# Making the moving operand's upper part ahead of the squares, the silu and the stationary operand's upper part, in a one-core decoder layer

## The chip, the cores and the metric

The kernel runs on one core of one Trainium2 chip. Five engines of the core take part: TensorE (PE; its weight loads are listed as PEld), VectorE (DVE), ScalarE (ACT), GpSimd (POOL) and SyncE (SP, which here only issues transfers). Each engine works through its own instructions in the order in which the program holds them, and semaphores tell one engine that another is done. The metric is the device time of one execution in microseconds; lower is better.

## The reference, cut to what matters

The reference is one inference step of a decoder layer for a prompt of 2048 tokens and for 32 sample tokens, in float32: a mixer of gated linear attention and a state-space part, then a cross-attention to 256 memory rows, then a SwiGLU feed-forward part, each with a norm before and after.

```python
def decoder_layer(x, s_gla, s_ssm, conv_buf, mk, mv, lw):
    m, s_gla, s_ssm, conv_buf = mixer(rmsnorm(x, lw['ln_mix_pre']), s_gla, s_ssm, conv_buf, lw)
    h = x + rmsnorm(m, lw['ln_mix_post'])
    a = cross_attend(rmsnorm(h, lw['ln_xa_pre']), mk, mv, lw['w_xq'], lw['w_xo'])
    h = h + rmsnorm(a, lw['ln_xa_post'])
    hf = rmsnorm(h, lw['ln_ffn_pre'])
    f = (jax.nn.silu(hf @ lw['w_gate']) * (hf @ lw['w_up'])) @ lw['w_down']
    h = h + rmsnorm(f, lw['ln_ffn_post'])
    return h, s_gla, s_ssm, conv_buf
```

The change concerns the dense products behind the mixer: `w_out`, the scores and values of the cross-attention (with weights folded beforehand), `w_gate` and `w_up`, and `w_down`.

## The kernel before, in words

**Products of three.** A float32 operand is split into an upper part, a copy of it in the type `fp32r`, and a lower part, the rest. ScalarE makes the upper part with a copy, VectorE the lower part with a subtraction that reads the upper one. `three` (lines 135 to 137) multiplies upper by upper, upper by lower and lower by upper: three matmuls for each block of 128 rows of contraction.

**Seven products for eight.** Each big product is cut in quarters, and seven products of sums of quarters give the four results (Winograd's form of Strassen's method). One such product is a **step** here: 12 matmuls with a contraction of 512, or 9 where it is 384. The stationary side of a step comes from a **unit** (class `Unit`): it loads a raw tile `raw`, VectorE makes sums `sum` (line 1650), ScalarE the upper part `s` (line 1668), VectorE the lower part, again `s` (line 1670). The moving side is kept in seven **places**, one for each product, made of **pieces** (class `Pieces`): a transfer issued by SP into a staging tile `st` (three of them; lines 1778 and 1795), the upper part on ScalarE (`larger`, line 1739, tile `r`), the lower part on VectorE, or on GpSimd for some (`smaller`, line 1743, tiles `r` or `e`); `smaller` then issues the load that lies three pieces ahead. A place takes two pieces.

**Passes.** `passes` lists nine passes of steps: `o`, `s`, `v` (mixer output, scores, values), three of `g` (gate and up for three blocks of rows) and three of `d` (down). The places stay for a whole pass and all units run past them. At the change from one pass to the next the seven places are made anew: while the last unit of a pass runs, one piece follows each step, and while the first unit of the next pass runs, again one piece follows each step. So there are nine stretches with 14 pieces each, and no pieces in between; in the first one seven of the 14 are made ahead of the loop.

**The order of the work.** `order` lists the steps by hand. For each step the loop of the function issues, in this order: the matmuls; the evacuation `evs` of the bank of PSUM (a copy on ScalarE for three of the seven products and the last, an addition on VectorE for the others: lines 1848 and 1850, 1977 and 1981, 1995 and 2002, 2047 and 2049); the functions in `later`, which are the squares of a finished half row (lines 1854 and 2056) or the silu (line 1982), and read what VectorE has just added; `part(e + 4)`, which gives VectorE the lower part for the step three ahead, and then the sum and ScalarE the upper part `s` for the step four ahead; `larger` of the piece; `tick`, the next bit of the norms and transposes of finished rows; and `smaller` of the piece. `pin` fixes this order on each engine. Some work is left loose (the sample rows' attention, line 1429, with its loads `sraw`, line 1418) and is set in between by the scheduler.

Of the kernel before, what the change touches and what calls it, by code (L numbers as in the profile page):

```python
# [42 lines left out]
def hymba_kernel(ctx: ExitStack, tc: tile.TileContext, a: dict, o: dict, dbg: dict | None = None):  # L43
# [1502 lines left out]
    def stage():  # L1546
        return pst.tile([P, 1024], F32, name="st", bufs=3)
# [269 lines left out]
    def rows(j, m):  # L1817
        return slice((2 * j + m) * P, (2 * j + m + 1) * P)
# [151 lines left out]
    def evac_gate(sg, w):  # L1970
        def ev(name, ps):
            i = AT[KEEP.get(name, name)]
            if i not in sg:
                sg[i] = pg.tile([P, 384], F32, name="sg", bufs=5)
            t = sg[i][:, 0:w]
            if name in KEEP:
                nc.scalar.copy(t, ps[:, 0:w])
            elif name == "C21":
                nc.scalar.activation(t, ps[:, 0:w], AF.Silu)
            else:  # L1980
                nc.vector.tensor_tensor(t, ps[:, 0:w], t, op=ALU.add)
                later.append(lambda: nc.scalar.activation(t, t, AF.Silu))
        return ev

    def evac_up(sg, w, blk, u):
        t3 = {}
        js = BLOCKS[blk]
        n = len(js)
        og = pg.tile([P, 1536], F32, name="og")[:, 0:n * 512].rearrange("p (j q c) -> p j q c", q=4, c=P)
        by = lambda x: x[:, 0:n * P].rearrange("p (j c) -> p j c", c=P)  # L1990

        def ev(name, ps):
            if name in KEEP:
                t = t3[KEEP[name]] = pg.tile([P, 384], F32, name="t", bufs=3)
                nc.scalar.copy(t[:, 0:w], ps[:, 0:w])
                return
            i = AT[name]
            s = sg[i]
            t = ps
            if name != "C21":  # L2000
                t = t3[name]
                nc.vector.tensor_tensor(t[:, 0:w], ps[:, 0:w], t[:, 0:w], op=ALU.add)
            nc.vector.tensor_tensor(og[:, :, i], by(t), by(s), op=ALU.mult)
            if w > n * P:
                nc.vector.tensor_tensor(s_f[:, 2 * u + i // 2, i % 2], t[:, n * P:w], s[:, n * P:w], op=ALU.mult)
            if name == "C21":
                if w > n * P:
                    there[0] = u + 1
                nc.gpsimd.dma_start(out=aT[js[0]:js[0] + n, :, u].rearrange("j p c -> p j c"), in_=og.rearrange("p j q c -> p j (q c)"))
        return ev  # L2010
# [116 lines left out]
    work = [(k, g, len(gs) - n) for k, (_, _, gs) in enumerate(passes) for n, g in enumerate(gs)]  # L2127
    begins = [n == 0 or work[n - 1][0] != k for n, (k, _, _) in enumerate(work)]
    XG, GD = 3, 3 + len(BLOCKS)

    def pieces_of(k):
        kind, i, _ = passes[k]
        if kind == "g":
            return pieces_g(k, i)
        if kind == "d":
            return pieces_w(k, a["w_down"], wT, *PARTS[i])
        return pieces_w(k, *{"o": (a["w_out"], wX[0]), "s": (flat2(wqk), wX[1]), "v": (flat2(wvo), wX[2])}[kind], 0, 4)
# [9 lines left out]
    def enter(k):  # L2147

        nonlocal pg, pd
        kind, i, _ = passes[k]  # L2150
        rate[:] = RATES[kind]
        if kind == "o":
            gain_row(px, "ln_mix_post")
            for u in range(4):
                aux.append(weight_sums(lambda n, u=u: flat2(wqk)[n, u], wX[1], u))
        if kind == "s":
            for u in range(4):
                aux.append(weight_sums(lambda n, u=u: flat2(wvo)[n, u], wX[2], u))
        if kind == "v":
            gain_row(px, "ln_xa_post")  # L2160
        if kind == "g":
            if i == 0:
                rctx.close()
                pg = fctx.enter_context(tc.tile_pool(name="pg", bufs=1, reuse_waits="tile"))

                pg.tile([P, 1536], F32, name="og")
            for u in range(NU):
                if u % (len(BLOCKS) - 1) == i:
                    aux.append(weight_sums(lambda n, u=u: a["w_down"][n, u], wT, u))
            if i + 1 == len(BLOCKS):  # L2170
                aux.append(samples_down())
        if kind == "d" and i == 0:
            fctx.close()
            pd = ctx.enter_context(tc.tile_pool(name="pd", bufs=1, reuse_waits="tile"))
            pd.tile([P, D], F32, name="m")
            pd.tile([P, D], F32, name="ga")
# [16 lines left out]
    def before_loads(k):  # L2193

        nonlocal rd
        kind, i, _ = passes[k]
        if kind != "g" or i + 1 < len(BLOCKS):
            drain(aux)
        if kind == "g" and i + 2 == len(BLOCKS):
            pin()  # L2200
            drain(back)
            pin(True)
            rd = ctx.enter_context(tc.tile_pool(name="rd", bufs=1, side="right", reuse_waits="tile"))
# [30 lines left out]
    coming = None  # L2234
    parted = 0

    for what in "sFsFsLFsFsFUsUFsUFsUPPFPPs":
# [4 lines left out]
        elif what == "L":  # L2242
            now = pieces_of(0)
# [28 lines left out]
    for e, (n, i) in enumerate(order):  # L2272
        k, g, left = work[n]
        kind, b, gs = passes[k]
        if i == 0:
            cur = n
            if begins[n]:
                if coming:
                    now, coming = coming, None
                enter(k)  # L2280
            held[n] = now
            w = now.w
            if kind == "g":
                if g[1] == 0:
                    sg = {}
                evs[n] = evac_gate(sg, w) if g[1] == 0 else evac_up(sg, w, b, g[0])
            elif kind == "d":
                h = {}
                if n + 1 == len(work):
                    for m in range(2):  # L2290
                        h[m] = stage()
                        nc.sync.dma_start(out=h[m], in_=hX[rows(g, m)])
                top = n in ys
                y = ys.pop(n, {})
                stays = left == 1 and b + 1 < len(PARTS)
                if stays:
                    ys[n + 1] = y
                evs[n] = evac_d(b, g, y, h, top, stays)
            else:
                evs[n] = quads(g, *{"o": (after_mix, True), "s": (after_scores, False), "v": (after_values, True)}[kind])  # L2300
            if left == 2 and k + 1 < len(passes):
                before_loads(k)
                coming = pieces_of(k + 1)
        if i == 2 and n + 1 < len(work) and on_top(n + 1):

            ys[n + 1] = {}
            for m in range(2):
                ys[n + 1][m] = pd.tile([P, D], F32, name="y", bufs=6)
                nc.sync.dma_start(out=ys[n + 1][m], in_=yp[work[n + 1][1]][:, m * D:(m + 1) * D])

        nt = PARTS[b][1] if kind == "d" else 4
        w = held[n].w
        if i == 0:
            banks[n, "A"] = accA.tile([P, 512], F32, name="accA")
        if i == 1:
            banks[n, "B"] = accB.tile([P, 512], F32, name="accB")
        if i == 3:
            banks[n, "C"] = accC.tile([P, 512], F32, name="accC")
        ps = banks[n, {1: "B", 3: "C", 5: "C"}.get(i, "A")]
        while i not in held[n].full:  # L2320
            held[n].step()
        sh, sl = units[n].got[i]
        start = i in (0, 1, 3)
        for kt in range(nt):
            ks = slice(kt * P, (kt + 1) * P)
            three(ps[:, 0:w], sh[:, ks], sl[:, ks], *held[n].moving(i, kt), start and kt == 0, kt == nt - 1, not start)
        if left == 1:
            spent.add((k, i))
        evs[n](NAMES[i], ps)

        todo, later[:] = list(later), []
        for fn in todo:
            fn()
        part(e + ahead_)

        p = coming if work[cur][2] == 1 else now if begins[cur] else None
        if p:
            p.larger()
        tick()
        if p:  # L2340
            p.smaller()
        if kind == "d" or not coming and now.done() and (k != XG or samp2):
            due[1] += rate[1]
            while due[1] >= 10:
                due[1] -= 10
                step(aux)
        pin()
        due[0] += rate[0]
        while due[0] >= 10:
            due[0] -= 10  # L2350
            step(back)
        pin(True)
        if samp2 is None and k == XG and not posts:
            leave_attention()
# [99 lines left out]
```

## Time and profile before

| what | value |
|---|---|
| time, median of 3 runs | 2816.3 us (2814.36 to 2820.68) |
| time of the profiled execution | 2820.75 us |
| its span, from the first to the last instruction | 2819.0 us |
| PE, DVE, ACT, POOL busy | 2729.5, 2079.1, 1472.8, 536.8 us |
| chain that ended last | PE 75%, DVE 13%, ACT 5%, DMA 3%, issue 3%, POOL 1% |
| upper parts of pieces, line 1739 | 126, of which 98 are 128x1024 |
| upper parts of the stationary operand, line 1668 | 798 |

A row of a group gives what the instruction writes and reads, how many there are, their busy time, the mean of one and, behind the second bar, how long the engine stood idle before them and for whom. In the time line a bracket at the end of a row is the idle time of that engine just before, with the instruction whose end released it. Steps, stretches and engines are named below as in this section.

### The profile page before, as it was taken

The numbers are of one execution on the slowest core, as the hardware profiler recorded it, in microseconds if no ns is written. First come the engines' busy times: TensorE is split into PE (matmuls) and PEld (weight loads), VectorE is DVE, ScalarE is ACT, GpSimd is POOL, SyncE is SP. The second block draws the span as 40 slices with busy tenths as digits, with TensorE's granted clock in tenths as the row PEclk, the third lists the DMA queues.
The fourth block names the chain that finished last, engine by engine and source line by source line (L and its number), as shares of the span: only waits on it lengthen the run. The fifth ranks groups of instructions, "written<-read, shape, count | busy, mean of one in ns | idle before, by whom it ended". The sixth has DMA issues, their size and how long they took to land.

```text
span 2819.0 us, 41809 instructions
## 1 busy us (share of the span) xinstructions
PE 2729.5 (97%) x15207; PEld 2367.6 (84%) x15207; DVE 2079.1 (74%) x3831; ACT 1472.8 (52%) x2921; POOL 536.8 (19%) x722
## 2 busy tenths in 40 slices
PE   8999999999998999999899999999999999999998
PEld 8987888788886878878799888899998998788786
DVE  7676677776757787677888787667678878574776
ACT  5545554554546787777755434434445555353432
POOL 2142332321321321015321210001000001000011
PEclk9999999999999999999999999999999999999999
DMA  7345435343266785468864567775234436464765
GB/s 255 113 142 188 148 106 160 118 131 90 83 215 226 282 291 223 146 189 254 263 222 179 177 237 243 253 254 178 98 137 171 156 120 209 168 219 99 239 152 132
DMA packets 151102, 512.17 MB, mean 182 GB/s; under 512 B 18176, under 2 KB 29488, under 8 KB 137328
## 3 DMA queue, kind: packets, MB, share of 16 engines
q1 hardware_dynamic: 94560, 331.81, 36.0%
q0 software_dynamic: 44240, 152.82, 16.8%
q10 hardware_dynamic: 12096, 24.86, 2.7%
q8 instruction: 120, 1.97, 0.3%
q14 instruction: 86, 0.70, 0.1%
HBM read 365.76 MB, written 143.67 MB: 181 GB/s over the span
## 4 chain that ended last, share of the span: by engine, by line
PE 75%; DVE 13%; ACT 5%; DMA 3%; issue 3%; POOL 1%; DVEq 0%; ACTq 0%; SPq 0%; POOLq 0%
PE accA L135 9%; PE accA L136 9%; PE accA L137 9%; PE accC L135 5%; PE accC L136 5%; PE accC L137 5%; PE acc L135 5%; PE acc L136 5%; PE acc L137 5%; PE accB L135 2%; PE accB L137 2%; PE accB L136 2%; DVE s L1670 2%; DVE sum L1650 2%; ACT r L1739 1%
## 5 line engine op out<-in xcount | busy, mean ns | idle before, releaser
L135 PE MATMUL accA<-r,s 128*128 128x512 f32 (+2 forms) x1792 | 637.2, 356 | 19.0 <-ACT r L1739 7.2
L137 PE MATMUL accA<-r,s 128*128 128x512 f32 (+2 forms) x1792 | 629.1, 351 | 2.9 <-DVE s L1670 2.8
L136 PE MATMUL accA<-r,s 128*128 128x384 f32 (+2 forms) x1472 | 502.7, 342 | 2.4 <-DVE r L1743 2.4
L135 PEld LDWEIGHTS accA<-r,s 128*128 128x128 f32 x1792 | 339.2, 189 | 70.9 <-ACT r L1739 11.0
L1668 ACT ACTIVATE s<-sum 128x512 fp32r<-128x512 f32 (+1 forms) x456 | 282.5, 620 | 218.9 <-DVE sum L1650 105.0
L137 PEld LDWEIGHTS accA<-r,s 128*128 128x128 f32 x1792 | 339.7, 190 | 33.2 <-DVE s L1670 4.0
L135 PE MATMUL accC<-r,s 128*128 128x512 f32 (+2 forms) x896 | 318.8, 356 | 9.2 <-ACT s L1668 3.2
L1670 DVE TENSOR_TENSOR s<-sum,s 128x512 fp32r<-128x512 f32 (+1 forms) x456 | 306.8, 679 | 20.1 <-ACT s L1668 19.8
L137 PE MATMUL accC<-r,s 128*128 128x512 f32 (+2 forms) x896 | 314.3, 351 | 0.0
L136 PEld LDWEIGHTS accA<-r,s 128*128 128x128 f32 x1472 | 279.0, 190 | 19.2 <-DVE r L1743 3.6
L1670 DVE TENSOR_TENSOR s<-raw,s 128x512 fp32r<-128x512 f32 (+1 forms) x342 | 233.7, 683 | 52.0 <-ACT s L1668 50.9
L136 PE MATMUL accC<-r,s 128*128 128x384 f32 (+2 forms) x736 | 251.3, 341 | 0.5 <-DVE r L1743 0.5
L1668 ACT ACTIVATE s<-raw 128x512 fp32r<-128x512 f32 (+1 forms) x342 | 213.3, 624 | 72.1 <-PE accC L137 49.8
L129 ACT ACTIVATE whi<-wraw 128x1024 fp32r<-128x1024 f32 (+2 forms) x140 | 128.9, 934 | 184.2 <-PE acc L136 104.5
L135 PEld LDWEIGHTS accC<-r,s 128*128 128x128 f32 x896 | 169.8, 189 | 37.2 <-ACT s L1668 7.8
L130 DVE TENSOR_TENSOR wlo<-wraw,whi 128x1024 fp32r<-128x1024 f32 (+2 forms) x140 | 156.2, 1127 | 48.0 <-ACT whi L129 47.3
L137 PEld LDWEIGHTS accC<-r,s 128*128 128x128 f32 x896 | 169.7, 189 | 14.9 <-DVE s L1670 0.2
L143 POOL TENSOR_TENSOR rs<-ms,nhalf 128x1 f32<-128x1 f32 (+4 forms) x125 | 111.0, 889 | 360.3 <-DVE ms L141 343.9
L135 PE MATMUL acc<-xhl,whi 128*128 128x512 f32 (+1 forms) x464 | 168.1, 363 | 8.3 <-ACT xhl L294 8.2
L137 PE MATMUL acc<-xhl,wlo 128*128 128x512 f32 (+1 forms) x464 | 164.3, 355 | 1.7 <-DVE wlo L130 1.7
L136 PE MATMUL acc<-xhl,whi 128*128 128x512 f32 (+1 forms) x464 | 164.1, 355 | 0.2 <-DVE xhl L295 0.2
L1650 DVE TENSOR_TENSOR sum<-raw 128x512 f32<-128x512 f32 (+1 forms) x228 | 156.4, 686 | 3.6
(696 smaller groups left out, 5857.9 us busy)
## 6 DMA issues: line engine op xcount, KB each, us to landing
raw<-in_w_gu_dram SPq DMA_DIRECT2D x66, 1024.0 KB, 4.9
wraw<-in_w_in_fm_dram SPq DMA_DIRECT2D x52, 512.0 KB, 3.6
wraw<-in_w_in_tm_dram SPq DMA_DIRECT2D x48, 512.0 KB, 3.9
st<-in_w_down_dram SPq DMA_DIRECT2D x37, 512.0 KB, 6.2
aT<-og POOLq DMA_DIRECT2D x22, 768.0 KB, 4.6
raw<-aT SPq DMA_DIRECT2D x16, 1024.0 KB, 6.3
out_y_dram<-y POOLq DMA_DIRECT2D x28, 512.0 KB, 6.1
yp<-y POOLq DMA_DIRECT2D x28, 512.0 KB, 6.6
```

Source lines behind the costliest of these rows:

```text
L129: last[0] = nc.scalar.activation(hi[:, cs], raw[:, cs], AF.Copy)
L130: nc.vector.tensor_tensor(lo[:, cs], raw[:, cs], f(hi)[:, cs], op=ALU.subtract)
L135: nc.tensor.matmul(ps, lhsT=wh, rhs=ah, start=start, stop=False, skip_group_check=more)
L136: nc.tensor.matmul(ps, lhsT=wh, rhs=al, start=False, stop=False, skip_group_check=more)
L137: nc.tensor.matmul(ps, lhsT=wl, rhs=ah, start=False, stop=stop, skip_group_check=more)
L143: nc.gpsimd.tensor_tensor(out=rs[:rows, :cols], in0=ms[:rows, :cols], in1=nhalf[:rows, :cols], op=ALU.pow)
L1650: nc.vector.tensor_tensor(t[out], x, y, op=o)
L1668: nc.scalar.activation(h3, v, AF.Copy)
L1670: return lambda: nc.vector.tensor_tensor(l3, v, f(h3), op=ALU.subtract)
L1739: nc.scalar.activation(hi, v, AF.Copy)
```

## The change

In each step of the nine stretches the piece's `larger` is issued right behind the evacuation, ahead of the functions in `later` and of `part`. `smaller` stays where it was. No instruction is added or removed by it.

```diff
         evs[n](NAMES[i], ps)
 
+        p = coming if work[cur][2] == 1 else now if begins[cur] else None
+        if p:
+            p.larger()
         todo, later[:] = list(later), []
         for fn in todo:
             fn()
         part(e + ahead_)
-
-        p = coming if work[cur][2] == 1 else now if begins[cur] else None
-        if p:
-            p.larger()
         tick()
         if p:
             p.smaller()
```

On ScalarE at the first stretch (pass `o`; `y<-accA` and `y<-accC` are evacuations, `mx,sq` a square, `s` the stationary operand's upper part, `r` a piece's):

```order
 L1848 COPY y<-accA 128x512
-L1668 ACTIVATE s<-sum 128x512
 L1739 ACTIVATE r_8234<-st 128x1024
+L1668 ACTIVATE s<-sum 128x512
+L1739 ACTIVATE r_8281<-st 128x1024
 L1854 ACTIVATE mx,sq_8256<-y 128x512
 L1668 ACTIVATE s<-sum 128x512
-L1739 ACTIVATE r_8286<-st 128x1024
```

The piece that stood behind the square and the next `s` stands ahead of both; the order of the others among themselves is the same.

On ScalarE in the last stretch, at the change to the third `d` pass, around the first square (`mx,sq`), before:

```order
L1668 ACTIVATE s<-sum 128x512
L1739 ACTIVATE r_25812<-st 128x1024
L2056 ACTIVATE mx,sq_25769<-y 128x512
L1668 ACTIVATE s<-sum 128x512
L1739 ACTIVATE r_25812<-st 128x1024
L1668 ACTIVATE s<-raw 128x512
L1739 ACTIVATE r_25858<-st 128x1024
L1668 ACTIVATE s<-raw 128x512
```

and with the change:

```order
L1739 ACTIVATE r_25807<-st 128x1024
L1668 ACTIVATE s<-sum 128x512
L1739 ACTIVATE r_25807<-st 128x1024
L2056 ACTIVATE mx,sq_25769<-y 128x512
L1668 ACTIVATE s<-sum 128x512
L1739 ACTIVATE r_25855<-st 128x1024
L1668 ACTIVATE s<-raw 128x512
L1739 ACTIVATE r_25855<-st 128x1024
```

Two pieces of one place now stand ahead of the square, with one `s` between them; before, the second stood behind the square and its `s`.

On PE the order of the steps is the same. One group of the loose work is set elsewhere: the five matmuls of the sample scores (`mx<-sraw,sqm`) in the stretch at the change to the second `g` pass. Before:

```order
L136 MATMUL accA<-r_17215,s 128x384
L137 MATMUL accA<-r_17215,s 128x384
L1429 MATMUL mx<-sraw,sqm 32x256 x5
L135 MATMUL accC<-r_17277,s 128x384
L136 MATMUL accC<-r_17277,s 128x384
```

and with the change:

```order
L137 MATMUL accC<-r_17272,s 128x384
L135 MATMUL accA<-r_17319,s 128x384
L1429 MATMUL mx<-sraw,sqm 32x256 x5
L136 MATMUL accA<-r_17319,s 128x384
L137 MATMUL accA<-r_17319,s 128x384
```

They stood ahead of the step into `accC` and now stand behind it and behind the first matmul of the next step.

## The prediction

> **What bounds the kernel now.** I read the table of stretches first, then the waits at the pieces' lines, then the time line at the worst places. Columns of the table: window and its length, busy us (and count) of PE, PEld, DVE, ACT and POOL, granted TensorE clock, DMA share, GB/s. The nine windows are the changes of pass; the tenth lies between two of them.
>
> ```profile
> span 2819.0 us, 41809 instructions
> ...
> 855.00:889.00 34.00, 26.47 (x79) 17.78 (x78) 22.34 (x29) 17.53 (x27) 1.44 (x1) 0.80 0.73 247
> 1012.00:1062.00 50.00, 45.16 (x208) 35.51 (x207) 45.45 (x63) 43.09 (x80) 12.89 (x16) 1.00 0.90 301
> 1186.00:1234.00 48.00, 45.99 (x215) 36.88 (x214) 41.05 (x61) 43.12 (x93) 2.49 (x5) 1.00 0.64 219
> 1354.00:1398.00 44.00, 36.14 (x173) 30.74 (x172) 38.69 (x67) 36.45 (x80) 17.49 (x27) 0.95 0.85 284
> 1741.00:1786.00 45.00, 41.41 (x279) 34.74 (x272) 35.39 (x55) 23.40 (x40) 0.76 (x1) 0.96 0.90 308
> 2095.00:2131.00 36.00, 30.11 (x187) 28.98 (x187) 29.25 (x49) 20.76 (x41) 0.74 (x1) 0.95 0.64 216
> 2351.00:2385.00 34.00, 28.39 (x155) 23.03 (x155) 28.48 (x43) 20.23 (x35) 10.17 (x9) 0.95 0.68 224
> 2481.00:2514.00 33.00, 31.71 (x139) 25.65 (x138) 30.53 (x40) 23.37 (x32) 1.06 (x2) 1.00 0.80 261
> 2630.00:2677.00 47.00, 42.74 (x179) 34.23 (x178) 39.27 (x53) 24.70 (x36) 1.42 (x2) 0.96 0.76 236
> 1100.00:1180.00 80.00, 80.00 (x387) 66.93 (x386) 52.05 (x91) 54.33 (x137) 8.62 (x16) 1.00 0.45 171
> ```
>
> Between changes PE is busy for 80.00 of 80 us: there PE bounds and nothing on ScalarE matters. The nine stretches last 371 us, and PE is busy for 328.1 of them (the column's sum), so 42.9 us are idle; and at a clock of 0.80, 0.95, 0.96, 0.95, 0.95 and 0.96 in six of them another 16 us or so are lost to half clock (34 x 0.20 = 6.8, 44 x 0.05 = 2.2, 45 x 0.04 = 1.8, 36 x 0.05 = 1.8, 34 x 0.05 = 1.7, 47 x 0.04 = 1.9). All that the change can win lies in these 59 us; it reaches only what hangs on the pieces. Which part that is, the views of lines 1739 (first rows) and 1743 (last two rows) tell: duration, what ScalarE idled for ahead of a piece, and who idled for it.
>
> ```profile
> L1739 ACT ACTIVATE r<-st x126: 239/1046/1110, 838.0 to 2673.5; 128x1024 fp32r<-128x1024 f32 x98, 128x512 fp32r<-128x512 f32 x21, 128x64 fp32r<-128x64 f32 x7
> ...
>   DMA st<-wX: 6.4, 4
>   DMA st<-in_w_down_dram: 3.8, 3
>   DMA st<-wT: 3.6, 6
>   DMA st<-xp: 1.8, 1
> ...
>   PE accA L135: 7.2, 7
> ...
>   ACT r L1739: 76.6, 62
> ...
>   PE accA L136: 9.6, 12
> ```
>
> VectorE and GpSimd stand idle for 76.6 us before lower parts because the upper part is not there yet, and PE waits 7.2 + 9.6 = 16.8 us directly, in 19 waits, for one or the other. ScalarE, on the other hand, waits for a piece's load in only 14 cases, 15.6 us (6.4 + 3.8 + 3.6 + 1.8).
>
> **The change, step by step.** It removes and adds nothing: the same copy of 1.05 us is issued earlier. What it moves past is seen in the third stretch (ScalarE, VectorE, PE in turn):
>
> ```profile
> 1228.51 0.60 ACT L1854 ACTIVATE mx<-y 128x512 f32<-128x512 f32 x1 [1.10 <-DVE y L1850]
> 1229.14 0.62 ACT L1668 ACTIVATE s<-sum 128x512 fp32r<-128x512 f32 x1
> 1229.66 1.04 ACT L1739 ACTIVATE r<-st 128x1024 fp32r<-128x1024 f32 x1
> ...
> 1228.99 0.68 DVE L1650 TENSOR_TENSOR sum<-sum,raw 128x512 f32<-128x512 f32 x1
> 1230.73 1.23 DVE L1743 TENSOR_TENSOR e<-st,r 128x1024 fp32r<-128x1024 f32 x1 [1.06 <-ACT r L1739]
> ...
> 1230.76 0.50 PE L135 MATMUL accA<-r,s 128*128 128x512 f32 x1 [0.49 <-ACT r L1739]
> 1232.02 0.50 PE L136 MATMUL accA<-e,s 128*128 128x512 f32 x1 [0.76 <-DVE e L1743]
> ```
>
> The piece stands 1.15 us behind the square's start (1229.66 - 1228.51), and the square itself waited 1.10 us for VectorE. If the load is there, the piece can run in that gap, at 1227.4. VectorE's order is unchanged, so its subtraction then follows its own sum, at 1229.7 in place of 1230.73: 1.06 us earlier, its whole wait. PE's first wait goes; the second shrinks, and together PE gets about 1.1 us. Where only the `s` copy stands ahead (1229.66 - 1229.14), it is 0.5 us. The cost moves to the square and `s`: they come 1.05 us later at most, but `s` is for the step four ahead, and a square's sum is read steps later.
>
> *Term 1, direct waits.* 19 waits come mostly in such pairs, so some ten places; one or two hang on the load. Nine places by 0.5 to 1.1 us are 4.5 to 9.9; I take **7 us**, nearer the row above, as most sit in steps with a square or silu.
>
> *Term 2, waits for a bank.* Where VectorE waits for a late piece, the next evacuation queues behind it. The last stretch shows that at its largest (same three engines):
>
> ```profile
> 2655.76 1.06 ACT L1739 ACTIVATE r<-st 128x1024 fp32r<-128x1024 f32 x1 [2.34 <-DMA st<-in_w_down_dram]
> 2658.71 0.60 ACT L2056 ACTIVATE mx<-y 128x512 f32<-128x512 f32 x1 [1.89 <-DVE y L2049]
> 2659.86 1.04 ACT L1739 ACTIVATE r<-st 128x1024 fp32r<-128x1024 f32 x1
> ...
> 2656.85 1.23 DVE L1743 TENSOR_TENSOR r<-st,r 128x1024 fp32r<-128x1024 f32 x1 [1.12 <-ACT r L1739]
> 2660.94 1.23 DVE L1743 TENSOR_TENSOR e<-st,r 128x1024 fp32r<-128x1024 f32 x1 [1.66 <-ACT r L1739]
> 2662.08 0.68 DVE L2049 TENSOR_TENSOR y<-accC,y 128x512 f32<-128x512 f32 x1
> ...
> 2662.91 0.52 PE L135 MATMUL accC<-r,s 128*128 128x512 f32 x1 [3.23 <-ACT s L1668]
> 2663.23 0.63 PE L136 MATMUL accC<-r,s 128*128 128x512 f32 x1
> 2663.66 0.63 PE L137 MATMUL accC<-r,s 128*128 128x512 f32 x1
> ```
>
> PE's wait of 3.23 us is put down to `s`, but `accC` was also being emptied until 2662.76. The piece at 2655.76 waits for its load and stays. The next one waited behind a square that waited for VectorE, which had waited for the first: by the new order it starts at about 2657.4 (behind one `s` of 0.6), is done before VectorE wants it, and VectorE saves its 1.66 us. PE gets 1.7 of the 3.23. Two more such waits end on ScalarE's own evacuations behind a piece:
>
> ```profile
> PE accC L135 <- ACT sg L1977: 3.0, 2, 2.1
> PE accC L135 <- ACT t L1995: 1.5, 1, 1.5
> PE mx L1429 <- DMA sraw<-in_cache_k_dram: 3.0, 1, 3.0
> ```
>
> Of their 4.5 us perhaps half goes, 2.3, since the silu or copy there waits for VectorE too: 1.7 + 2.3 = **4 us**, bounds 1 and 6.
>
> *Term 3, half clock.* At 2663.23 and 2663.66 matmuls start 0.43 us apart; that is how half the clock looks, and it follows the long wait. The stretch 1012:1062 idles for 4.84 us in shorter waits and stays at 1.00. Of the 16 us I take **3**; bounds 0 and 8 (half, as the first stretch's waits begin with loads). [...]
>
> *Term 4, the loose group.* PE's 3.0 us for `sraw` (last row above) stood ahead of a step of 12 matmuls that did not need it; that step now runs during the load, until the next one waits for its own piece. **2 us**, bounds -1 (the other sample loads come later) and 3.
>
> *Term 5, the charge.* A piece in front that waits for its load now holds the square, `s` and the next evacuation.
>
> ```profile
> 1051.14 0.61 ACT L1668 ACTIVATE s<-raw 128x512 fp32r<-128x512 f32 x1
> 1054.57 1.06 ACT L1739 ACTIVATE r<-st 128x1024 fp32r<-128x1024 f32 x1 [2.81 <-DMA st<-wX]
> ```
>
> Here `s` slips from 1051.14 to 1055.6, 4.5 us; PE needs it four steps on, 12 matmuls a step, so it is nearly covered. Fourteen such pieces each cost what follows at most 0.6 to 1.2 us of copies formerly done during the wait: 0 to 17 us if all reached PE; I take **3**, since only evacuations have no slack.
>
> *Term 6, absorption.* A gain of one step is lost where VectorE is simply full: 30.53 busy of 33 us in 2481:2514, 45.45 of 50 in 1012:1062. **3 us**, bounds 0 and 7.
>
> Sum: 7 + 4 + 3 + 2 - 3 - 3 = **10 us**. The profiled execution took 2820.75 us (span 2819.0 and 1.75 around it), 4.45 above the median of 2816.3; the same 10 us on the median give **2806 us**. With all bounds at their bad ends it is 4.5 + 1 + 0 - 1 - 17 - 7 = -19.5, at their good ends 9.9 + 6 + 8 + 3 = 27.
>
> **The rivals.** *A, VectorE or the loads are the bound of a change of pass (no difference).* With three staging tiles a load can only be issued when the piece three before it is subtracted, so an earlier piece just waits for its load, and VectorE's queue stays full. For it: the VectorE shares just named, DMA shares up to 0.90. Against it: 76.6 us of waits for the upper part against 15.6 us of ScalarE's for loads. Terms 1 to 3 then give about 4 and term 5 takes 2 back: 2814 us.
>
> *B, the queue blocks (slower).* One mechanism: the piece in front waits for `st`, and the evacuation behind it keeps `accC` or `accA` full. The place is the `wX` and `w_down` loads (the 2.81 and 2.34 us above). It decides once `s` is late by over three steps, 3 x 12 x 0.22 = 8 us (0.22 us from one matmul to the next is half of the 0.43 above), or an evacuation by over one, 2.6 us; 1.05 + 2.81 = 3.9 is past the second. With 1.2 us at each of 14 pieces, 17 us of waits less 7 for term 1, it is 10 us slower: 2826 us. [...]
>
> [...]
>
> The order of the instructions shows that the piece does move ahead, so that it does nothing is not a rival.
>
> **How the numbers follow.** Forecast 0.55, A 0.24, B 0.11, C 0.10. A measurement of this kernel tells 0.2% from no change, 5.6 us: faster means below 2810.7. Nearly all of C, 0.50 of the forecast and 0.05 of A lie there: 0.65. Slower is B, above 2821.9: 0.10. Within: 0.25. The forecast's own range is 2798 to 2812; for 8 in 10 it reaches into A and C: 2796 to 2817.
>
> **What would show it.** Right: the idle time of VectorE for line 1739 falls from 76.6 us to under 40; PE's 16.8 us at least halves; the wait of 3.23 us falls under 2; the clock of 855:889 rises above 0.85; the rows between changes stay as they are. Wrong: ScalarE's waits for `st` grow by as much as VectorE's fall (A), or PE waits for evacuations and `s` behind a piece that waits for its load (B). What would upset it all is that pieces become ready earlier and the load of three later does not.

## The result and the profile after

| | before | changed |
|---|---|---|
| median of 4 runs | 2815.33 us (2810.73 to 2820.68) | 2794.44 us (2789.85 to 2797.14) |
| ratio to before | 1 | 0.9919 [0.9907, 0.9931] |
| profiled execution | 2820.75 us, span 2819.0 | 2795.36 us, span 2793.6 |

The change makes the kernel 20.9 us faster, 0.8%. The forecast had the direction, but less than half of the size: 10 us, 2806 us, and even its wide range (2796 to 2817) ends 1.6 us above what was measured.

The page of the changed kernel, its span and the shares of the chain that ended last:

```profile
span 2793.6 us, 41826 instructions
...
PE 78%; DVE 11%; ACT 4%; issue 3%; DMA 3%; POOL 1%; DVEq 0%; POOLq 0%; SPq 0%; ACTq 0%
```

In the chain PE has gone from 75% to 78%, and VectorE from 13% to 11%.

**Where the time went.** To compare the stretches, each is cut in both traces at the same two instructions of VectorE (lower parts of the stationary operand, line 1670, which stand in the same place of the order in both). The table of windows gives for each its length, then PE's busy time, and behind the busy times of the other engines the granted clock. Before, the first stretch (change to `o`), the first of `g`, the last of `d`, and the sum over all nine:

```profile
865.30:909.30 44.00, 39.34 (x147) 29.86 (x147) 31.40 (x50) 25.91 (x52) 6.92 (x10) 0.86 0.54 183
...
1351.00:1415.10 64.10, 56.24 (x286) 50.27 (x285) 54.92 (x94) 48.59 (x103) 22.16 (x34) 0.95 0.77 256
...
2625.00:2679.40 54.40, 50.14 (x211) 40.32 (x210) 45.06 (x62) 25.52 (x37) 2.47 (x4) 0.97 0.73 222
sum 479.80, PE 439.79 PEld 366.35 DVE 397.43 ACT 312.81 POOL 68.91; mean PE 48.87 PEld 40.71 DVE 44.16 ACT 34.76 POOL 7.66
```

and the same with the change:

```profile
862.30:900.60 38.30, 35.62 (x147) 26.94 (x147) 31.13 (x51) 25.43 (x52) 6.16 (x10) 0.97 0.60 215
...
1336.60:1401.30 64.70, 57.15 (x286) 51.32 (x285) 54.40 (x93) 48.47 (x103) 23.70 (x34) 0.92 0.76 254
...
2604.80:2654.00 49.20, 48.25 (x212) 39.22 (x211) 44.71 (x62) 25.62 (x37) 3.37 (x4) 1.00 0.80 245
sum 459.20, PE 433.54 PEld 363.49 DVE 395.03 ACT 311.88 POOL 71.20; mean PE 48.17 PEld 40.39 DVE 43.89 ACT 34.65 POOL 7.91
```

All nine, from the same two tables (PE idle is length less PE busy):

| stretch | length, us | difference | PE idle, us | clock |
|---|---|---|---|---|
| `o` | 44.0 to 38.3 | -5.7 | 4.7 to 2.7 | 0.86 to 0.97 |
| `s` | 72.3 to 69.3 | -3.0 | 4.8 to 2.5 | 1.00, 1.00 |
| `v` | 54.3 to 51.7 | -2.6 | 2.0 to 0.3 | 1.00, 1.00 |
| `g`, first | 64.1 to 64.7 | +0.6 | 7.9 to 7.6 | 0.95 to 0.92 |
| `g`, second | 52.7 to 50.8 | -1.9 | 3.6 to 2.8 | 0.97 to 0.93 |
| `g`, third | 43.1 to 39.5 | -3.6 | 5.9 to 2.8 | 0.96, 0.96 |
| `d`, first | 53.5 to 53.8 | +0.3 | 5.6 to 4.7 | 0.97 to 0.94 |
| `d`, second | 41.4 to 41.9 | +0.5 | 1.3 to 1.3 | 1.00, 1.00 |
| `d`, third | 54.4 to 49.2 | -5.2 | 4.3 to 1.0 | 0.97 to 1.00 |
| sum | 479.8 to 459.2 | -20.6 | 40.0 to 25.7 | |

Of the 20.6 us, 14.3 are idle time of PE and 6.3 are busy time, of which 3.7 lie in the first stretch, where the clock rises. Of the 25.4 us between the two spans, 3.0 more lie ahead of the first cut, where executions differ by chance (the cut is at 865.2 in a second profile of the changed kernel, and at 861.3 in a kernel tried below that keeps the old order there), and 1.8 lie between the stretches; the medians leave 20.9. Three stretches gain nothing, in the second profile as in the first.

The view of line 1739 in the changed kernel, what ScalarE idled for ahead of a piece and who idled for it (us, times), and the last rows from the view of line 1743, the lower part:

```profile
  DMA st<-wT: 19.9, 18
  DMA st<-xp: 15.8, 9
  DMA st<-wX: 8.7, 6
  DMA st<-in_w_down_dram: 8.7, 4
...
  DVE r L1743: 24.1, 27
  POOL r L1743: 24.1, 6
...
  DVE e L1743: 6.2, 6
  PE accA L135: 5.8, 4
...
  ACT r L1739: 54.4, 39
...
  PE accA L136: 7.2, 10
```

Before, the waits for an upper part were these:

```profile
  DVE r L1743: 39.9, 45
  POOL r L1743: 25.9, 6
...
  DVE e L1743: 10.9, 11
```

VectorE's own waits fall from 50.8 to 30.3 us, GpSimd's six stay at 24.1. ScalarE's waits for loads of pieces grow from 15.6 us in 14 cases to 54.6 in 39 (the four rows, and 1.0 and 0.5 us in two more), the sign that was named for rival A, and yet the kernel is faster.

**The last stretch**, where the bank of `accC` had kept PE for 3.23 us. ScalarE, VectorE and PE in turn, with the change:

```profile
2634.89 1.06 ACT L1739 ACTIVATE r<-st 128x1024 fp32r<-128x1024 f32 x1 [4.83 <-DMA st<-in_w_down_dram]
...
2636.38 1.04 ACT L1739 ACTIVATE r<-st 128x1024 fp32r<-128x1024 f32 x1
2637.85 0.60 ACT L2056 ACTIVATE mx<-y 128x512 f32<-128x512 f32 x1 [0.42 <-DVE y L2049]
...
2635.99 1.23 DVE L1743 TENSOR_TENSOR r<-st,r 128x1024 fp32r<-128x1024 f32 x1 [0.55 <-ACT r L1739]
...
2638.33 1.22 DVE L1743 TENSOR_TENSOR e<-st,r 128x1024 fp32r<-128x1024 f32 x1
...
2640.29 0.47 PE L135 MATMUL accC<-r,s 128*128 128x512 f32 x1 [0.86 <-DVE y L2049]
2640.60 0.40 PE L136 MATMUL accC<-r,s 128*128 128x512 f32 x1
2640.83 0.40 PE L137 MATMUL accC<-r,s 128*128 128x512 f32 x1
```

The second piece starts 1.5 us behind the first, ahead of the square, where 4.1 lay between them before. VectorE's subtraction at 2638.33 waits for nothing (1.66 before), the bank comes free earlier, PE's wait is 0.86, and the matmuls behind it stand 0.23 us apart, not 0.43 (before, the trace's granted clock is 0.50 from 2663.18 to 2666.59). The first piece's wait for its load, now 4.83, kept nobody on PE.

**The first stretch** shows the busy time that went. PE before:

```profile
863.60 0.51 PE L135 MATMUL accA<-r,s 128*128 128x512 f32 x1 [1.34 <-ACT r L1739]
864.86 0.79 PE L136 MATMUL accA<-e,s 128*128 128x512 f32 x1 [0.76 <-DVE e L1743]
...
868.15 0.80 PE L135 MATMUL accC<-r,s 128*128 128x512 f32 x1 [0.79 <-ACT y L1848]
...
874.23 0.57 PE L136 MATMUL accA<-r,s 128*128 128x512 f32 x1
874.63 0.39 PE L137 MATMUL accA<-r,s 128*128 128x512 f32 x1
```

and with the change:

```profile
860.54 0.49 PE L135 MATMUL accA<-r,s 128*128 128x512 f32 x1 [1.79 <-ACT r L1739]
861.80 0.79 PE L136 MATMUL accA<-e,s 128*128 128x512 f32 x1 [0.76 <-DVE e L1743]
...
864.80 0.46 PE L136 MATMUL accC<-r,s 128*128 128x512 f32 x1
865.10 0.40 PE L137 MATMUL accC<-r,s 128*128 128x512 f32 x1
```

In both, the granted clock falls to 0.50 in the second wait of the same pair, at 864.36 us before and at 861.51 with the change. Before, one more wait followed, 0.79 us for ScalarE's evacuation, and matmuls stayed slow from 864.86 to 874.23, 9.4 us; with the change that wait is not there and they are slow from 861.80 to 864.80, 3.0 us. That this wait decides how long the slow spell lasts is not shown. In the second profile of the changed kernel, which lacks the wait too, the clock of this stretch is 0.93; and in a kernel tried below (the three stretches that gain nothing), which keeps the old order here and such a wait, it is 0.96:

```profile
865.10:907.40 42.30, 35.66 (x147) 27.33 (x146) 31.44 (x50) 25.84 (x52) 6.97 (x10) 0.96 0.53 191
```

With this higher clock and the old order PE is busy for 35.7 us in place of 39.3, but idle for 6.6 in place of 4.7, and the stretch is only 1.7 us shorter than before. So in this stretch about half of what the clock saves comes back as longer waits, and a loss reckoned from the clock alone overstates what the clock costs here.

### The profile page after: what moved, and what is told of

Same layout as the page of the kernel before. It is cut to its first block, busy times and chain, and to the rows that moved or that the text cites. A ratio compares the mean times of both kernels' runs of the same rounds, so it can differ in the third digit from the quotient of the medians.

```text
span 2793.6 us, 41826 instructions
## 1 busy us (share of the span) xinstructions
PE 2720.1 (97%) x15207; PEld 2362.1 (85%) x15207; DVE 2075.6 (74%) x3831; ACT 1472.2 (53%) x2921; POOL 540.1 (19%) x722
## 3 DMA queue, kind: packets, MB, share of 16 engines
q0 software_dynamic: 44240, 152.82, 16.8%
## 4 chain that ended last, share of the span: by engine, by line
PE 78%; DVE 11%; ACT 4%; issue 3%; DMA 3%; POOL 1%; DVEq 0%; POOLq 0%; SPq 0%; ACTq 0%
PE accA L135 10%; PE accA L136 10%; PE accA L137 10%; PE accC L135 5%; PE acc L135 5%; PE accC L137 5%; PE accC L136 5%; PE acc L136 5%; PE acc L137 5%; PE accB L135 3%; PE accB L137 3%; PE accB L136 3%; DVE s L1670 2%; DVE sum L1650 1%; PE mx L1863 1%
```

## The experiments

The theory behind the prediction is that a piece in front takes waits from VectorE and PE, and that it is charged for each load that ScalarE then waits for. The experiments put the new order into some stretches, move the piece past the one or the other, and make the loads later. Times are medians, ratios are to the kernel before on the same chip in the same set of runs (medians 2816.7, 2815.9 and 2816.6 us in the three sets).

### Half of the stretches each

```diff
-        if p:
+        soon = p and p.k < XG
+        if soon:
             p.larger()
         todo, later[:] = list(later), []
         for fn in todo:
             fn()
         part(e + ahead_)
+        if p and not soon:
+            p.larger()
```

This is the changed kernel with the new order in the changes to `o`, `s` and `v` alone; its counterpart has `p.k >= XG`, the six changes to `g` and `d`.

> The piece is issued in front only in the stretches at the changes into the passes o, s and v; in the six others it stays behind. Theory (each stretch wins what its late pieces cost, on its own): the two profiles lose 11.3 us between them in these three stretches (5.7, 3.1, 2.5), so 11 us faster than before, about 2804. Rival (the gain is that of the half clock, in the first and the last stretch): 6 us faster, 2809. Rival (some of the 21 us is the chance of the runs): under 5 us.

> The converse: in front in the stretches into the three g and the three d passes, behind in o, s and v. Theory: the profiles give 9.3 us here (g2 3.6, the last d 5.2, the second g 1.9, the other three lose 1.5 together), so 9 to 10 us faster than before, about 2806, and with the run beside it the two add up to the whole change, 20 to 22 us. Rival (half clock alone): 5 us, the last stretch. If they do not add up, a stretch's gain depends on the one before.

Measured: 2804.93 us, ratio 0.996 [0.9945, 0.9975], for `o`, `s`, `v`; 2805.98, 0.9964 [0.9949, 0.9978], for `g` and `d`. The gains, 11.8 and 10.7 us, add up to 22.5, what the whole brings. Cut as above, the first kernel's three stretches are 4.4, 2.7 and 2.5 us shorter, and in the second the gain lies in the second and third `g` and the last `d` (3.1, 3.2 and 5.7). The stretches that keep the old order are 0.8 us longer in sum in the first kernel and 0.6 shorter in the second, though one of them alone can differ by more (the last `d` of the first kernel is 2.4 shorter). So most of the gain is local to each stretch, and PE's wait for `sraw` (4.2 us in the first kernel, none in the second) goes with the change at `g` alone.

### The three stretches that gain nothing

```diff
-        soon = p and p.k < XG
+        soon = p and p.k in (XG, GD, GD + 1)
```

The new order stands only in the first change to `g` and the first two to `d`.

> The piece in front only in the stretches into the first g pass and into the first and second d pass, where the profiles of the whole change gain nothing (0.6, 0.4 and 0.5 us longer). Theory (VectorE's queue is full there, so an earlier piece only waits: term 6): between 2 us slower and 2 us faster than before. Rival (they gain as the others do, and the profiles of single executions hide it): 4 us or more faster.

Measured: 2814.37 us, 0.9991 [0.9983, 1.0], 2.3 us faster, just beyond what the theory allowed and short of the rival's 4. Those three stretches are 0.5 us shorter, 0.4 longer and 1.6 longer than before. There a third of the pieces moves ahead for next to nothing. The theory's reason, a full VectorE, does not tell these stretches from the others: in the table of windows before, VectorE is busy for 0.86, 0.82 and 0.90 of them, and for 0.87 of the changes to `s` and to `v`, which gain 3.0 and 2.6 us. What they show is this: in the first `g` and the first `d` PE's longest wait is for an evacuation by VectorE, and it stays (3.4 and 4.1 us before, 3.8 and 3.6 with the whole change); in the second `d` PE idles for only 1.3 us to begin with. Why those two waits stay was not tried. The whole again, beside it on the same chip:

> The changed kernel itself, timed beside the next one: 20 to 24 us faster than before.

Measured: 2795.65 us, 0.9923 [0.991, 0.9935]; the result repeats.

### Past the squares only, past `s` only

```diff
         p = coming if work[cur][2] == 1 else now if begins[cur] else None
+        part(e + ahead_)
         if p:
             p.larger()
         todo, later[:] = list(later), []
         for fn in todo:
             fn()
-        part(e + ahead_)
```

This puts the piece behind `s` but ahead of the squares and the silu. The other order has `later`, the piece, `part`: behind the squares, ahead of `s`.

> The piece goes behind the stationary operand's upper part but in front of the squares and silu, which therefore also come behind the stationary part. Theory: 8 to 14 us faster than before, about 2804, more than the run beside it, as the square's wait for VectorE is the longer one. Rival (the stationary part's wait for the sum holds the piece): under 5 us.

> The piece goes behind the squares and silu but in front of the stationary operand's upper part, in all nine stretches. Theory (what holds the piece is mostly the square or silu, which waits for VectorE's addition, plus 0.6 us of the stationary part): this part alone moves a piece by 0.5 us, so 5 to 8 us faster than before, about 2809. Rival (the stationary part holds it, since it waits for VectorE's sum): 15 us or more, with VectorE's wait for pieces falling as far as with the whole change.

Measured: past the squares only 2790.61 us, 0.9905 [0.9889, 0.9921]; past `s` only 2801.17, 0.9946 [0.9931, 0.9961]. The gains of 26 and 15.5 us do not add up to the whole's 21, and both are larger than was expected (8 to 14 and 5 to 8 us); the second is what its rival had named. Each of the two moves takes much of the same waits away: VectorE's own waits for an upper part, 50.8 us before and 30.3 with the whole change, are 36.9 past the squares only and 34.7 past `s` only. So the theory's split, by which mostly the squares hold the piece and `s` only a little, does not stand. Past the squares only comes out best, so it was run again:

> The order stationary part, piece, squares and silu once more, beside the changed kernel. If the stationary part in front costs the piece nothing (it was 3.8 us ahead of the changed kernel in another job), 2 to 6 us faster than the changed kernel; if that was chance, within 2 us of it.

Measured: 2789.2 us, 0.9906 [0.989, 0.9921], 6.4 us below the changed kernel beside it (4 us before; the intervals of the two overlap a little, but the sign is the same both times). It beats both kernels. It would be easy to read this as the charge for putting a piece that waits ahead of `s`. The windows speak against that for the larger part. In the profiles the lead is 9.4 us (spans 2793.6 and 2784.2), and the nine stretches hold 3.0 of it (459.3 against 456.3; 1.7 in the second pair of profiles). 6.0 us lie between the stretches, where no piece is made (5.6 in the second pair), 3.4 of them in the first `g` pass. Those windows, changed kernel and then past the squares only:

```profile
1401.30:1721.90 320.60, 313.76 (x1900) 291.45 (x1899) 264.63 (x556) 151.86 (x292) 53.58 (x79) 1.00 0.60 209
```

```profile
1396.60:1713.80 317.20, 311.88 (x1900) 291.34 (x1899) 261.42 (x556) 154.09 (x293) 52.52 (x79) 1.00 0.61 211
```

In that pass loose work on the state (`Ms`, line 1227) stands in VectorE's queue and waits for GpSimd, which waits for a load (6.61 us in the changed kernel at 1544.19, 6.55 in the other at 1539.28). The view of that line, what VectorE idled for, in the changed kernel and in the other:

```profile
  POOL Ms L1222: 3.4, 1
```

```profile
  POOL Ms L1222: 1.0, 1
```

Behind it PE waits 1.57 us for a lower part `s` in the changed kernel and not at all there. This work is not pinned, and in these traces it comes at another time where the order is another. That it makes up these 3.4 us was read from the traces and not tried by itself; the rest, in the later `g` passes, was not followed.

### Loads one piece later

```diff
-        return Pieces(k, [[part(i, *c) for c in cuts] for i in range(7)], 512, 3, n == 4)
+        return Pieces(k, [[part(i, *c) for c in cuts] for i in range(7)], 512, 2, n == 4)
...
-        return Pieces(k, [[part(i, *c) for c in cuts] + ([sample_part(i)] if ws else []) for i in range(7)], w, 3)
+        return Pieces(k, [[part(i, *c) for c in cuts] + ([sample_part(i)] if ws else []) for i in range(7)], w, 2)
```

Each load of a piece is issued two pieces ahead in place of three, in the kernel before and in the changed one. If waiting for loads at the head of ScalarE's queue costs what Term 5 or rival B say, the change must be worth less here.

> The order of before, but a piece's load is issued two pieces ahead in place of three, so ScalarE finds fewer loads landed. This one prices late loads in the old order: a load takes 5 us and a step 2.7, so waits of about 1 to 3 us at most pieces; 10 to 40 us slower than before, 2826 to 2856. It is the base for the run beside it.

> The changed order with the loads two pieces ahead. Theory (the charge, term 5, is close to nothing, since a piece in front waits for its load in time in which ScalarE would wait for VectorE's addition or PE anyway): not slower than the run beside it, between 0 and 10 us faster. Term 5 as it was priced (up to 1.2 us behind each waiting piece that reaches PE), or rival B: with nearly all 126 pieces waiting, 10 us or more slower than the run beside it.

Measured: 2823.02 us, 1.0026 [1.0015, 1.0037], in the old order, less than was expected; 2798.63, 0.9944 [0.9928, 0.996], in the new one. The change is worth 24.4 us here, against 20.9 with early loads (by the ratios 23 both times), and not the 0 to 10 that were expected. ScalarE's waits in the new order (view of line 1739):

```profile
  DMA st<-wT: 27.6, 17
  DMA st<-xp: 19.9, 12
  DMA st<-wX: 10.5, 7
  DMA st<-in_w_down_dram: 5.2, 6
```

With 3.4 and 1.8 us in two more cases that is 68.4 us in place of 54.6, in 44 cases in place of 39. In the old order it is 28.0 us in 23 cases, in place of 15.6 in 14. So the later loads did not make nearly all pieces wait, as was expected, and the test is weaker than planned: both orders got 12 to 14 us more of such waits. By the ratios each loses about 7 us by them. A charge that the new order alone would pay does not show.

### Ahead of the evacuation too

```diff
-        evs[n](NAMES[i], ps)
-
         p = coming if work[cur][2] == 1 else now if begins[cur] else None
         if p:
             p.larger()
+        evs[n](NAMES[i], ps)
```

> The changed kernel with the piece one place further in front, ahead of the evacuation copy too. Theory (what counts is to be out of the squares' way; beyond that the piece waits for its load): 2790 to 2798, no different from the changed kernel by more than 4 us. Rival B (a piece that waits for its load holds the bank through the copy behind it): 5 us or more slower than the changed kernel, 2799 or more.

Measured: 2793.48 us, 0.9925 [0.9908, 0.9941], the changed kernel's time. PE's direct waits in the nine stretches, cut as above, fall further, to 6.9 us (15.3 before, 11.1 in the changed kernel), and its waits for banks grow, to 15.7 (11.5 in the changed kernel). The waits of PE in this kernel that end on evacuations by ScalarE:

```profile
PE accA L135 <- ACT y L1848: 5.2, 2, 4.8
PE accC L135 <- ACT sg L1977: 4.6, 4, 2.8
...
PE accA L135 <- ACT sg L1977: 3.0, 3, 1.6
```

So one thing behind a waiting piece does hold PE: an evacuation. Here 12.8 us of PE's waits end on ScalarE's copies (5.2 + 4.6 + 3.0), 2.8 in the changed kernel's first profile. Moving the piece past that point exchanges one wait for another, and the time stays.

### The lower part earlier as well

```diff
         for fn in todo:
             fn()
-        tick()
         if p:
             p.smaller()
+        tick()
```

The order past the squares only, with VectorE's lower part ahead of the norms and transposes (`tick`).

> The order stationary part, piece, squares and silu (the fastest so far, 2790.6) with VectorE's lower part of the piece issued ahead of the next bit of the norms and transposes in place of behind it. If VectorE's queue ahead of the lower part is what is left of the wait, 3 to 6 us faster than that, about 2786, since the load three ahead is issued earlier too; if the loads are the bound or the norms become late, 2789 to 2796.

Measured: 2799.95 us, 0.9952 [0.9935, 0.997]: 9 us slower than without it. That is more than either case of the expectation allowed. The profiles have it in the nine stretches (466.9 us against 456.3). PE's waits for banks are 15.1 us there in place of 11.1, and for the transposes' `u` and `mx` 6.3 in place of 3.8. So what is put in front on VectorE pushes back something that PE needs.

## Why the prediction was right in sign and half in size

In the changed kernel, two of PE's waits in this account are these (us, times, longest), and below them the second as it was before:

```profile
PE accC L135 <- ACT sg L1977: 2.8, 2, 1.9
...
PE mx L1863 <- ACT u L1906: 1.6, 2, 1.1
```

```profile
PE mx L1863 <- ACT u L1906: 3.8, 4, 2.1
```

**Term 1, direct waits (+7), and Term 6, absorption (-3): together right in size.** The two groups went from 16.8 to 13.0 us (5.8 + 7.2), 3.8 less, in 14 waits in place of 19. One of the 14, of 2.83 us, is new and belongs to Term 4 (below); without it 6.6 us went. There are stretches in which the new order gains nothing (0.9991 [0.9983, 1.0] for the three alone), but the reason that Term 6 gave for them does not hold: of the two stretches that it named for a full VectorE, the second `d` gains nothing and `s` gains 3.0 us.

**Term 2, waits for a bank (+4): right for the waits that it named.** The 3.23 us became 0.86, the two for `sg` went from 3.0 to 2.8 (one of them, 0.8 us before and after, lies in the first `g` pass, where no piece is made), that of 1.5 for `t` is gone: 7.7 to 3.7. With all evacuations and the upper parts `s` in the nine stretches, PE's waits fell from 17.0 to 11.5 us, by 5.5, which is 1.5 more than the term.

**Term 4, the loose group (+2): its wait went, and another took most of its place.** PE no longer waits for `sraw` (3.0 us), and the step that stood behind it runs at once; but the step after that now waits for a piece that waits for its load:

```profile
1756.05 0.69 PE L135 MATMUL accA<-r,s 128*128 128x384 f32 x1 [2.83 <-ACT r L1739]
```

The term had said so: the step runs until the next one waits for its own piece. The new wait is 1.95 us in the second profile. In all, PE's idle time in this stretch falls by 0.8 us (3.6 to 2.8), so the term brought less than 2.

**Term 5, the charge (-3, bounds 0 to 17): failed.** The step said that fourteen pieces each cost up to 1.2 us of copies formerly done during the wait, and took 3 us for them. There were 39 such waits, not fourteen, 54.6 us in all, and PE waits for no upper part `s` of line 1668 behind them but 0.1 us; the change gains as much with the loads two pieces ahead. What was overlooked: ScalarE is busy for 312 of the 459 us, and before, it idled ahead of the squares, the silu and `s`, mostly for results of VectorE and PE; now it idles ahead of its piece, for a load, and by then those results are mostly there. In the nine stretches its idle time ahead of squares, silu and `s` fell from 107.0 to 41.5 us, that ahead of pieces rose from 13.4 to 55.9, and all its idle time together fell from 164.5 to 144.4. So a wait has changed its place and not been added, and the term sits at its lower bound. The mechanism exists for an evacuation. In the second profile of the changed kernel it struck once: ScalarE and then PE in the first change to `g`,

```profile
1370.38 0.63 ACT L1739 ACTIVATE r<-st 128x512 fp32r<-128x512 f32 x1 [3.66 <-DMA st<-xp]
...
1374.28 0.48 ACT L1977 COPY sg<-accA 128x384 f32<-128x384 f32 x1
...
1374.81 0.44 PE L135 MATMUL accA<-r,s 128*128 128x384 f32 x1 [2.47 <-ACT sg L1977]
```

2.5 us, which the first profile does not have, since that load had come.

**Missing from the sum: the transposes.** PE's waits for `u` and `mx`, which hang on ScalarE's and VectorE's norms in the same stretches, fell from 4.8 to 2.2 us, 2.6 less (3.0 us are left in the second profile). That VectorE's queue, and with it `tick`, moves on sooner is the likely reason; it was not tried by itself. Against it stands a wait of 1.0 us for a lower part `s` in the first change to `d`, which both profiles of the changed kernel have and the one before has not.

**Term 3, half clock (+3, bounds 0 to 8): within its bounds, its size open.** By the clocks in the table of stretches, length times the missing share, half clock costs about 16 us before and 15 with the change, but only 9 in the second profile of the changed kernel (where the second change to `g` stands at 1.00, not 0.93), so a single trace can't give this term. Over all executions with a recorded clock, the mean granted clock is 0.9924 before (37 executions) and 0.9946 with the change (9): 0.0022 of 2805 us is 6 us. That is an upper bound for the term: the first stretch showed that part of what the clock saves comes back as waits, and some of it lies outside the stretches (the first `g` pass stands at 0.99 before and at 1.00 with the change). The reason given for a small value, that the first stretch's waits begin with loads, holds (the wait that starts it is still there, 1.79 us).

**The sum** as measured in PE's waits: 3.8 direct, 3.0 `sraw`, 5.5 banks and `s`, 2.6 transposes, less 1.0 for the lower part: 13.9 us, close to the 14.3 by which the table's idle time fell. The other 7 of the 20.9 us between the medians are busy time of PE (6.3 in the table), which the clock explains only in part. The forecast had 4 for direct waits, 2, 4, nothing for the transposes, -3 for the charge and 3 for the clock. So of the 10.9 us that it lacks, 3 are the charge that did not come, 1.6 the waits that were missing from it, 1.5 the banks and 0.8 the direct waits with `sraw`; the last 4 lie in PE's busy time and stay open.

**The rivals.** A (the bound is elsewhere) showed its sign, waits for loads that grow by 39 us, but not its time; with 14 us more of them the new order still gained 24.4. B (slower) is refuted in sign; its place of 2.81 and 2.34 us was right for the waits, and no wait of PE behind them shows, except at an evacuation. C stood for all 16 us of half clock in place of 3: 2793 us, the time nearly measured, but at most 6 us of half clock went in the whole span. No run shows that the clock stays up once the waits are short enough: before, it fell to 0.50 at 864.36 in the second of two waits, 1.34 and 0.76 us, and it stood at 1.00 from 1012 to 1062, over a wait of 1.57.

**What was to be seen.** Right: the wait of 3.23 us under 2 (0.86); the clock at 855 to 889 above 0.85 (0.86 to 0.97 in the stretch around it). Wrong: VectorE's idle time for line 1739 under 40 us (54.4), since 24.1 of it are six waits of GpSimd, which that row holds too and the change does not reach; VectorE's own are 30.3. Wrong too: PE's 16.8 us at least halved (13.0). The rows between the changes stay as they are within 0.4 us, but for the first two `g` passes (3.4 shorter and 1.6 longer).

## What to carry to other kernels

In this kernel ScalarE's waits for loads at the head of its queue grew by 39 us while the time fell by 20.9, and where PE waited for what stood behind them, it was for evacuations (2.47 us in one profile, and 12.8 us for ScalarE's copies with the piece ahead of them too). So ask of a new wait what the engine idled for in the old order (here mostly results of VectorE and PE: 107.0 us ahead of squares, silu and `s`, and 41.5 with the change), and charge only for what comes later than that, above all for evacuations. Where a stretch is made of many short waits of the matmul engine, sum all groups of waits there, not only those that carry the moved instruction's name, and take the clock from several executions (one stretch of one program stood at 0.93 in one profile here and at 1.00 in another). When one order beats another by a few microseconds, look first whether the difference lies in the place that was changed, since work that is not pinned moves along.

## What was not expected of the hardware

ScalarE's waits for loads grew from 15.6 to 54.6 us, and in one experiment to 68.4, while the kernel became faster by 20.9 and 24.4 us.

The half clock starts in the second of two waits, 1.34 and 0.76 us with one matmul between them (863.60 and 864.86 before), 1.79 and 0.76 with the change, while 4.84 us of waits in the 50 us from 1012 to 1062, the longest of 1.57, leave the clock at 1.00; and the matmuls became fast again after 9.4 us in the one and after 3.0 in the other. The same stretch of the same program stood at 0.93 in one profile and at 1.00 in another; why was not shown. In the traces' records of the granted clock, the spells at 0.50 last 3.41, 6.83 or 10.24 us, before (eight, one and one of them) as with the change (four, three and none), apart from the spell in each that reaches past the last instruction.

The second change to `g` in the second profile of the changed kernel (0.93 in the table above):

```profile
1725.00:1773.80 48.80, 45.73 (x311) 39.15 (x310) 39.29 (x63) 27.67 (x47) 0.76 (x1) 1.00 0.85 295
```
